# Feed-forward of a hybrid decoder trunk: the fourth weight sum of a seven-product pair written over its raw weights, t1 and t2 in units of their own

## The chip, the cores and the metric

The kernel runs on one core of a Trainium2 chip. Its time is device time in microseconds (us), the median of several executions. PE is the matrix engine (PEld its weight loads), DVE the vector engine, ACT the scalar engine, POOL GpSimd, and SP the queue that issues the weights' DMAs.

## The reference

Two layers over 256 positions of width 2048, all in float32: an mLSTM and state-space mixer in layer 0, block-sparse attention in layer 1, and after each a feed-forward of hidden width 5632, with norms and residuals around them. What the change touches is the feed-forward alone:

```python
def swiglu(x, w_gate, w_up, w_down):
    return (jax.nn.silu(x @ w_gate) * (x @ w_up)) @ w_down
...
    x = x + swiglu(rms_norm(x, norm_ffn[layer]), *ffn_params[layer])
```

## The kernel before

All weights stream once from HBM. A float32 product is done on PE in three passes: a weight is split into a rounded high part `wh` (a cast on ACT, L362) and the rest `wl` (a subtraction on DVE, L363), and activations are split in the same way, so that L399 to L401 multiply high with high, high with low, and low with high.

A feed-forward goes in three groups of 4, 4 and 3 hidden strips of 512 columns. For each strip `hidden` calls `block` with the gate and up weights; then `down` calls `block` twice, for q = 0 and q = 1, each with two strips of the down weights, and adds the four result banks to the residual `xres` (L865). A block walks in pairs of k tiles, after a plan of letters (PSPSPSPP for eight pairs, PSPSPP for six). Each pair needs two loads of 512 KB, raw a and raw b, of two k tiles each. A P pair is multiplied plainly: 24 matmuls. An S pair is done with seven products in place of eight (Strassen's scheme, in Winograd's form): 21 matmuls. It needs four sums of raw weights on DVE, here with the lines of before: L376 t1 = b(second half) - a(second half); L378 t3, over the second half of b; L379 t2, from b and t1; L381 t4, from a's first half and t2. t1 and t2 lie in one tile `sums`, t4 in half a tile `last`. a, b and `sums` are split whole, `last` by half.

Tiles come from rings of units of 4 KB for each partition. A unit is taken by turn and is free again once its last reader is done. Before, `raw` a, `raw` b, `sums` and `last` all take turns in one ring of eight units (tag raw0 four times, then raw1 four times); so an S pair takes four turns and a P pair two. `wh` and `wl` have rings of six each. A load can be issued when the unit of its turn is free, mostly after a split on DVE, and PE frees the `wh` and `wl` units. A list scheduler (Tile) puts all instructions of an engine in one fixed order when the kernel is built, by priorities and by when it thinks that units come free. SP, DVE, ACT and PE each run their own list in order; the first that must wait holds all behind it.

After the last S pair of a block come the pre-additions (L429 to L433) that free the four E banks. At the end of a block the four F banks are read by L865 (down) or by L850, L853 and L854 (hidden), before the next block's first products may write them.

Of the kernel before, what the change touches and what calls it, by code (L numbers as in the profile page):

```python
# [37 lines left out]
PLAN_H = {4: "PSPSPSPP", 3: "PSPSPP"}  # L38
MIXER = ({"wide": 2}, {"raw": 4, "wh": 3, "wl": 3}, {"blk": 8})
ATTN = ({"wide": 2}, {"qk": 8}, {"blk": 4}, {"raw": 4, "wh": 3, "wl": 3})  # L40
FFN = ({"raw0": 4}, {"wh0": 2}, {"wl0": 2}, {"raw1": 4, "wh1": 4, "wl1": 4}, {"skh": 3}, {"blk": 4})


def _host_constants():
# [15 lines left out]
def hybrid_trunk(ctx: ExitStack, tc: tile.TileContext, a: dict, out: bass.AP):  # L60
    nc = tc.nc
# [20 lines left out]
    def open_stage(name, pools):  # L82

        close_stage()
        stage["guards"], stage["pools"] = [], []
        for i, tags in enumerate(pools):
            guard = tc.tile_pool(name=f"{name}{i}", bufs=1, reuse_waits="tile")  # L90
            stage["guards"].append(guard)
            stage["pools"].append((guard.__enter__(), tags))

    def held_tile(tag, shape, name, dt=F32):
        for pool, tags in stage["pools"]:
            if tag in tags:
                return pool.tile(shape, dt, tag=tag, name=name, bufs=tags[tag])
        raise KeyError(tag)
# [254 lines left out]
    def weights(src, row, summed):  # L353

        def unit(kind, ring, name, dt=F32):
            turn[kind] = turn.get(kind, -1) + 1
            return held_tile(kind + ring[turn[kind] % len(ring)], [P, 2, STRIP], name, dt)

        def parts(of, n=2):
            h = unit("wh", "001111", "wh", F32R)  # L360
            l = unit("wl", "001111", "wl", F32R)
            nc.scalar.copy(h[:, :n, :], of[:, :n, :])  # L362
            nc.vector.tensor_sub(l[:, :n, :], of[:, :n, :], h[:, :n, :].bitcast(F32))  # L363
            return [(h[:, i, :], l[:, i, :]) for i in range(n)]

        raw = []
        for w, col in src:
            raw.append(unit("raw", "00001111", "raw"))
            nc.sync.dma_start(raw[-1], w[row:row + 2 * P, col:col + STRIP].rearrange("(a p) f -> p a f", p=P))
        with tc.high_priority(offset=800):  # L370
            if not summed:
                return [parts(r) for r in raw]
            a, b = raw
            sums = unit("raw", "00001111", "sums")
            last = unit("raw", "00001111", "last")
            nc.vector.tensor_sub(sums[:, 0, :], b[:, 1, :], a[:, 1, :])  # L376
            b21, b11 = parts(a)
            nc.vector.tensor_sub(b[:, 1, :], b[:, 0, :], b[:, 1, :])  # L378
            nc.vector.tensor_sub(sums[:, 1, :], b[:, 0, :], sums[:, 0, :])  # L379
            b22, t3 = parts(b)  # L380
            nc.vector.tensor_sub(last[:, 0, :], a[:, 0, :], sums[:, 1, :])  # L381
            t1, t2_ = parts(sums)
            t4, = parts(last, 1)
            return b21, b11, b22, t3, t1, t2_, t4

    def block(src, kt, row, nk, plan, after_sums=None, lead=1):
# [19 lines left out]
        for j in range(n):  # L406
            if plan[j] == "S":
                held[0] = True
                b21, b11, b22, t3, t1, t2_, t4 = weights(src, row + 2 * j * P, True)
                tok = lambda k, t: tuple(x[:, t * P:(t + 1) * P] for x in kt.parts(k))  # L410
                k2, k1 = 2 * j, 2 * j + 1
# [13 lines left out]
                if j == last_s:  # L425
# [8 lines left out]
                    if after_sums is not None:  # L434
                        after_sums(pre)
            else:
                group.append((j, weights(src, row + 2 * j * P, False)))
                if len(group) < lead and j < n - 1 and n - j <= lead:
                    continue
# [384 lines left out]
    def project_add(w, kt, nk, name, gcol):  # L824

        nx = KT("x" + name, KD, long)
        nx.sums = {j: None for j in range(KD // 2) if PLAN_X[j] == "S"}
        ss = cst.tile([P, NT, 4], F32, name="ss" + name)
        turn["acc"] = 4
        for s in range(4):  # L830
            banks = lin_a(w, s * STRIP, kt, nk)
            cs = slice(s * STRIP, (s + 1) * STRIP)
            for t in range(NT):
                nc.vector.tensor_add(xr_[t][:, cs], xr_[t][:, cs], banks[t])
            transpose_later(nx, s, [xr_[t][:, cs] for t in range(NT)], gcol, 1, 1 if s < 3 else 0)
            for t in range(NT):
                sumsq(ss[:, t, s:s + 1], xr_[t][:, cs])
        return nx, col_norm(name, ss)
# [51 lines left out]
    xt1, r1 = project_add(a["l0_w_out"], mixed, 32, "1", G_FFN0)  # L890
    open_stage("f", FFN)
    xt2 = KT("x2", KD, long)
# [44 lines left out]
    parts = (slice(0, P), slice(P, W3))  # L937
# [49 lines left out]
    xt3, r3 = project_add(a["l1_w_o"], oT, KD, "3", G_FFN1)  # L987
    open_stage("g", FFN)

# [56 lines left out]
```

## Time and profile before

| | us |
|---|---|
| median of 3 runs (2628.16 to 2630.83) | 2628.64 |
| the profiled execution, its time | 2630.54 |
| its span, first to last instruction | 2628.8 |
| first feed-forward, about | 783 to 1512 |
| second feed-forward with the tail, about | 1893 to 2629 |

A row of the waits says who waited, for whom, how long in total, how often, and the longest. A row of the timeline has start, duration, engine, line, operation, what it writes and reads, and in brackets how long the engine idled before it and what ended that. PE's matmuls overlap: one of 512 columns is listed with 0.39 us, but the next starts 0.23 us later. The granted PE clock is 0.997 of full speed over the whole span, and the 16 DMA engines are busy for 58% of each of the two feed-forwards.

### The profile page before, as it was taken

How to read it: one execution, taken by the hardware profiler on the slowest of the kernel's cores; microseconds unless marked ns; L12 is line 12 of the kernel's file. 1: busy time of each engine (PE TensorE's matmuls, PEld its weight loads, DVE VectorE, ACT ScalarE, POOL GpSimd, SP SyncE). 2: the span in 40 equal slices, each digit the busy share in tenths (PEclk: the TensorE clock that was granted, in tenths of full speed). 3: DMA queues.
4: the chain of work that ended last, by engine and by line, in shares of the span. 5: the costliest groups of instructions: out<-in, count | busy, mean ns of one | idle time of the engine just before them, and what ended most of it. 6: DMA issues, size and time to landing. Idle time of an engine off the chain costs nothing.

```text
span 2628.8 us, 33211 instructions
## 1 busy us (share of the span) xinstructions
PE 2581.6 (98%) x12231; PEld 2141.4 (81%) x12231; DVE 2069.3 (79%) x2768; ACT 1470.6 (56%) x2003; POOL 46.8 (2%) x97
## 2 busy tenths in 40 slices
PE   8999999999999999999999999999999999999998
PEld 7888888888887877787788788888888878887876
DVE  6675787765549998999899866566699889988998
ACT  5465665665446555555455556556565545554554
POOL 2000010000000000000000000000000000000000
PEclk9999999999999999999999999999999999999999
DMA  7566576566646655655565465555465556554654
GB/s 227 176 188 183 178 238 183 168 185 218 189 152 211 205 180 196 198 195 190 186 203 191 160 191 171 175 177 191 154 220 190 198 163 221 192 193 163 221 199 137
DMA packets 254771, 496.71 MB, mean 189 GB/s; under 512 B 15704, under 2 KB 16096, under 8 KB 254352
## 3 DMA queue, kind: packets, MB, share of 16 engines
q1 hardware_dynamic: 250816, 484.57, 57.7%
q0 software_dynamic: 2896, 8.51, 1.2%
q8 instruction: 96, 1.57, 0.2%
q10 hardware_dynamic: 896, 1.52, 0.2%
q14 instruction: 67, 0.55, 0.1%
HBM read 492.39 MB, written 2.14 MB: 188 GB/s over the span
## 4 chain that ended last, share of the span: by engine, by line
PE 74%; DVE 14%; DMA 6%; issue 4%; ACT 2%; SPq 0%; DVEq 0%; POOL 0%; ACTq 0%; POOLq 0%
PE acc_w L305 11%; PE acc_f L400 8%; PE acc_f L401 8%; PE acc_f L399 8%; PE acc_a L347 8%; PE acc_a L349 8%; PE acc_a L348 8%; DVE wl L363 7%; PE acc_w L309 6%; DMA raw<-in_l_ffn_down 3%; DMA raw<-in_l_ffn_up 3%; PE acc_e L399 2%; PE acc_e L401 2%; PE acc_e L400 2%; ACT wh L362 1%
## 5 line engine op out<-in xcount | busy, mean ns | idle before, releaser
L362 ACT CAST wh<-raw 128x1024 fp32r<-128x1024 f32 x528 | 546.0, 1053 | 416.8 <-PE acc_f L401 190.5
L290 DVE TENSOR_TENSOR wl<-raw,wh 128x1024 fp32r<-128x1024 f32 (+1 forms) x385 | 470.0, 1221 | 334.2 <-ACT wh L289 330.1
L363 DVE TENSOR_TENSOR wl<-raw,wh 128x1024 fp32r<-128x1024 f32 x528 | 636.7, 1223 | 86.0 <-ACT wh L362 82.7
L289 ACT CAST wh<-raw 128x1024 fp32r<-128x1024 f32 (+1 forms) x385 | 403.1, 1047 | 388.9 <-PE acc_a L349 175.7
L399 PE MATMUL acc_f<-wh,x 128*128 128x512 f32 x1012 | 396.1, 393 | 8.3 <-DVE xres L865 6.4
L401 PE MATMUL acc_f<-wh,x 128*128 128x512 f32 x1012 | 395.5, 391 | 0.0
L400 PE MATMUL acc_f<-wl,x 128*128 128x512 f32 x1012 | 395.4, 391 | 0.0
L399 PEld LDWEIGHTS acc_f<-wh,x 128*128 128x128 f32 x1012 | 190.1, 188 | 51.8 <-issue 8.0
L401 PEld LDWEIGHTS acc_f<-wh,x 128*128 128x128 f32 x1012 | 190.8, 189 | 39.7
L400 PEld LDWEIGHTS acc_f<-wl,x 128*128 128x128 f32 x1012 | 190.6, 188 | 39.1
L305 PE MATMUL acc_w<-xa,wh 128*128 128x512 f32 x768 | 209.5, 400 | 1.1 <-DVE xa L169 1.1
L305 PEld LDWEIGHTS acc_w<-xa,wh 128*128 128x128 f32 x768 | 140.1, 190 | 27.3 <-ACT wh L289 1.5
L347 PE MATMUL acc_a<-wh,xa 128*128 128x512 f32 x384 | 151.2, 394 | 0.0
L349 PE MATMUL acc_a<-wh,xa 128*128 128x512 f32 x384 | 151.0, 393 | 0.0
L348 PE MATMUL acc_a<-wl,xa 128*128 128x512 f32 x384 | 150.0, 391 | 0.0
L305 PE MATMUL acc_w<-x,wh 128*128 128x512 f32 x512 | 137.9, 399 | 0.0
L363 DVE TENSOR_TENSOR wl<-sums,wh 128x1024 fp32r<-128x1024 f32 x98 | 119.9, 1223 | 3.7 <-ACT wh L362 3.2
L309 PE MATMUL acc_w<-xa,wl 128*128 128x256 f32 x768 | 122.0, 283 | 0.0
L309 PEld LDWEIGHTS acc_w<-xa,wl 128*128 128x128 f32 x768 | 110.5, 191 | 6.7
L362 ACT CAST wh<-sums 128x1024 fp32r<-128x1024 f32 x98 | 102.7, 1048 | 15.3 <-PE acc_e L401 7.8
L305 PEld LDWEIGHTS acc_w<-x,wh 128*128 128x128 f32 x512 | 93.3, 189 | 17.7
L362 ACT CAST wh<-last 128x512 fp32r<-128x512 f32 x98 | 60.8, 620 | 82.5 <-DVE last L381 59.1
(318 smaller groups left out, 4768.5 us busy)
## 6 DMA issues: line engine op xcount, KB each, us to landing
raw<-in_l_w_in SPq DMA_DIRECT2D x191, 512.0 KB, 3.7
raw<-in_l_ffn_gate SPq DMA_DIRECT2D x176, 512.0 KB, 4.4
raw<-in_l_ffn_up SPq DMA_DIRECT2D x176, 512.0 KB, 4.9
raw<-in_l_ffn_down SPq DMA_DIRECT2D x176, 512.0 KB, 5.2
raw<-in_l_w_qkv SPq DMA_DIRECT2D x96, 512.0 KB, 3.6
raw<-in_l_w_out SPq DMA_DIRECT2D x64, 512.0 KB, 4.6
raw<-in_l_w_o SPq DMA_DIRECT2D x32, 512.0 KB, 4.0
rows<-scr POOLq DMA_DIRECT2D x10, 512.0 KB, 5.8
```

The lines of the kernel that those rows point to most:

```text
L289: nc.scalar.copy(wh[:, ks, :], raw[:, ks, :])
L290: nc.vector.tensor_sub(wl[:, ks, :], raw[:, ks, :], wh[:, ks, :].bitcast(F32))
L305: nc.tensor.matmul(banks[f], wh[:, kk, f * P:(f + 1) * P], kt.both(k0 + kk), start=k0 + kk == 0, stop=False, skip_group_check=True)
L309: nc.tensor.matmul(banks[f][:, :T], wl[:, kk, f * P:(f + 1) * P], kt.parts(k0 + kk)[0], start=False, stop=k0 + kk == nk - 1, skip_group_ch ...
L347: nc.tensor.matmul(banks[t], xh[:, ts], wh[:, kk, :], start=k == 0, stop=False)
L348: nc.tensor.matmul(banks[t], xh[:, ts], wl[:, kk, :], start=False, stop=False)
L349: nc.tensor.matmul(banks[t], xl[:, ts], wh[:, kk, :], start=False, stop=k == nk - 1)
L362: nc.scalar.copy(h[:, :n, :], of[:, :n, :])
L363: nc.vector.tensor_sub(l[:, :n, :], of[:, :n, :], h[:, :n, :].bitcast(F32))
L399: nc.tensor.matmul(dst, ah, bh, start=start, stop=False)
L400: nc.tensor.matmul(dst, ah, bl, start=False, stop=False)
L401: nc.tensor.matmul(dst, al, bh, start=False, stop=stop)
```

## The change

`last` goes: t4 is written over the first half of a, and split from there. `sums` gets two units of its own, and the raw ring keeps six. The eight units of 4 KB stay eight. One line fewer stands in the code, so L376, L378, L379, L381 and L865 of before are L375, L377, L378, L380 and L864 now.

```diff
-FFN = ({"raw0": 4}, {"wh0": 2}, {"wl0": 2}, {"raw1": 4, "wh1": 4, "wl1": 4}, {"skh": 3}, {"blk": 4})
+FFN = ({"raw0": 4}, {"wh0": 2}, {"wl0": 2}, {"raw1": 2, "sum0": 2, "wh1": 4, "wl1": 4}, {"skh": 3}, {"blk": 4})
...
         for w, col in src:
-            raw.append(unit("raw", "00001111", "raw"))
+            raw.append(unit("raw", "000011", "raw"))
...
             a, b = raw
-            sums = unit("raw", "00001111", "sums")
-            last = unit("raw", "00001111", "last")
+            sums = unit("sum", "0", "sums")
             nc.vector.tensor_sub(sums[:, 0, :], b[:, 1, :], a[:, 1, :])
             b21, b11 = parts(a)
             nc.vector.tensor_sub(b[:, 1, :], b[:, 0, :], b[:, 1, :])
             nc.vector.tensor_sub(sums[:, 1, :], b[:, 0, :], sums[:, 0, :])
             b22, t3 = parts(b)
-            nc.vector.tensor_sub(last[:, 0, :], a[:, 0, :], sums[:, 1, :])
+            nc.vector.tensor_sub(a[:, 0, :], a[:, 0, :], sums[:, 1, :])
             t1, t2_ = parts(sums)
-            t4, = parts(last, 1)
+            t4, = parts(a, 1)
```

What the scheduler makes of it is seen in the lists of the engines. The numbers in the names rise in the order in which the code makes the tiles.

The first place is SP's list in the second feed-forward, first group, q = 1: the loads of its fifth to eighth pairs. Before:

```order
L369 DMA raw_18525<-in_l1_ffn_down 128x2x512
L369 DMA raw_18527<-in_l1_ffn_down 128x2x512
L369 DMA raw_18561<-in_l1_ffn_down 128x2x512
L369 DMA raw_18563<-in_l1_ffn_down 128x2x512
L369 DMA raw_18657<-in_l1_ffn_down 128x2x512
L369 DMA raw_18659<-in_l1_ffn_down 128x2x512
L369 DMA raw_18621<-in_l1_ffn_down 128x2x512
L369 DMA raw_18623<-in_l1_ffn_down 128x2x512
```

And the same loads now:

```order
L369 DMA raw_18459<-in_l1_ffn_down 128x2x512
L369 DMA raw_18461<-in_l1_ffn_down 128x2x512
L369 DMA raw_18495<-in_l1_ffn_down 128x2x512
L369 DMA raw_18497<-in_l1_ffn_down 128x2x512
L369 DMA raw_18554<-in_l1_ffn_down 128x2x512
L369 DMA raw_18556<-in_l1_ffn_down 128x2x512
L369 DMA raw_18590<-in_l1_ffn_down 128x2x512
L369 DMA raw_18592<-in_l1_ffn_down 128x2x512
```

Before, the eighth pair's loads (18657, 18659) stand ahead of the seventh's (18621, 18623); now each load stands in the order of its use.

The second place is DVE's list in the first feed-forward, first group, q = 1, about its fourth to sixth pairs (the fourth and sixth are S pairs). Before, from the split of raw 8949 (third pair), whose end lets the load of raw 9068 (sixth pair) be issued, to the split of raw 8985 (b of the fourth pair):

```order
L363 TENSOR_TENSOR wl_8956<-raw_8949,wh_8955 128x1024
L363 TENSOR_TENSOR wl_8991<-raw_8983,wh_8990 128x1024
L381 TENSOR_TENSOR last_8988<-raw_8983,sums_8987 128x512
L363 TENSOR_TENSOR wl_9002<-sums_8987,wh_9001 128x1024
L363 TENSOR_TENSOR wl_9006<-last_8988,wh_9005 128x512
L376 TENSOR_TENSOR sums_9070<-raw_9068,raw_9066 128x512
L865 TENSOR_TENSOR xres1_5690<-xres1_5690,pre_8770 128x512
L363 TENSOR_TENSOR wl_8997<-raw_8985,wh_8996 128x1024
```

The same now, from the split of raw 8933, which lets raw 9051 be loaded:

```order
L363 TENSOR_TENSOR wl_8940<-raw_8933,wh_8939 128x1024
L363 TENSOR_TENSOR wl_8974<-raw_8967,wh_8973 128x1024
L380 TENSOR_TENSOR raw_8967<-raw_8967,sums_8971 128x512
L363 TENSOR_TENSOR wl_8980<-raw_8969,wh_8979 128x1024
L363 TENSOR_TENSOR wl_8989<-raw_8967,wh_8988 128x512
L363 TENSOR_TENSOR wl_9018<-raw_9013,wh_9017 128x1024
L375 TENSOR_TENSOR sums_9053<-raw_9051,raw_9049 128x512
```

The fourth pair's b (raw 8985, now 8969) was split behind the first sum of the sixth pair; now it is split ahead of it, with t4 and a split of the fifth pair.

The third place is DVE's list in the first feed-forward, last group, where q = 0 ends and q = 1 has begun: the residual's sums over q = 0 and the second and fourth pairs of q = 1. Before:

```order
L865 TENSOR_TENSOR xres0_5689<-xres0_5689,pre_12660 128x512
L363 TENSOR_TENSOR wl_12820<-raw_12808,wh_12819 128x1024
L865 TENSOR_TENSOR xres0_5689<-xres0_5689,acc_f_12496 128x512
L381 TENSOR_TENSOR last_12811<-raw_12806,sums_12810 128x512
L363 TENSOR_TENSOR wl_12825<-sums_12810,wh_12824 128x1024
L363 TENSOR_TENSOR wl_12829<-last_12811,wh_12828 128x512
L376 TENSOR_TENSOR sums_12897<-raw_12895,raw_12893 128x512
L865 TENSOR_TENSOR xres1_5690<-xres1_5690,pre_12661 128x512
L378 TENSOR_TENSOR raw_12895<-raw_12895 128x512
L865 TENSOR_TENSOR xres1_5690<-xres1_5690,acc_f_12489 128x512
L363 TENSOR_TENSOR wl_12901<-raw_12893,wh_12900 128x1024
```

And now, from the fourth pair's first sum on:

```order
L375 TENSOR_TENSOR sums_12849<-raw_12847,raw_12845 128x512
L363 TENSOR_TENSOR wl_12772<-raw_12761,wh_12771 128x1024
L380 TENSOR_TENSOR raw_12759<-raw_12759,sums_12763 128x512
L363 TENSOR_TENSOR wl_12777<-sums_12763,wh_12776 128x1024
L363 TENSOR_TENSOR wl_12781<-raw_12759,wh_12780 128x512
L377 TENSOR_TENSOR raw_12847<-raw_12847 128x512
L378 TENSOR_TENSOR sums_12849<-raw_12847,sums_12849 128x512
L864 TENSOR_TENSOR xres0_5689<-xres0_5689,pre_12613 128x512
L363 TENSOR_TENSOR wl_12852<-raw_12845,wh_12851 128x1024
L864 TENSOR_TENSOR xres0_5689<-xres0_5689,acc_f_12451 128x512
L380 TENSOR_TENSOR raw_12845<-raw_12845,sums_12849 128x512
L864 TENSOR_TENSOR xres1_5690<-xres1_5690,pre_12614 128x512
```

The fourth pair's first sum and the splits of t1, t2 and t4 stood between the residual's sums or behind two of them; now they stand ahead of all three rows with `xres` that are shown. Two more sums of `xres1`, the second over an F bank (acc_f_12444), follow directly.

## The prediction

> **What bounds the kernel now.** I read the page's engine row first, then the stretches of the two feed-forwards, and then who PE waits for in each.
>
> ```profile
> span 2628.8 us, 33211 instructions
> PE 2581.6 (98%) x12231; PEld 2141.4 (81%) x12231; DVE 2069.3 (79%) x2768; ACT 1470.6 (56%) x2003; POOL 46.8 (2%) x97
> 783.00:1512.00 729.00, 714.48 (x3168) 581.43 (x3167) 657.43 (x826) 406.28 (x477) 1.38 (x2) 1.00 0.58 191
> 1893.00:2629.00 736.00, 712.77 (x3136) 578.63 (x3134) 658.75 (x826) 403.86 (x468) 1.79 (x3) 0.99 0.58 190
> ```
>
> PE sets the time. The change touches only the two feed-forwards (the last two rows: length, then busy time of PE, PEld, DVE, ACT, POOL), and there PE idles 729.0 - 714.5 = 14.5 us and 736.0 - 712.8 = 23.2 us, the second with the kernel's tail in it. No change to the weights' buffers can bring more than these 37.7 us. What PE waits for (us in total, times, longest), three rows of the first feed-forward and the largest of the second:
>
> ```profile
> PE acc_f L400 <- DVE wl L363: 4.7, 2, 3.0
> PE p_tr L223 <- DVE h L854: 3.5, 5, 1.1
> ...
> PE acc_f L399 <- DVE xres L865: 0.8, 3, 0.3
> ...
> PE acc_f L399 <- DVE xres L865: 7.2, 9, 2.1
> ```
>
> Only the first row is a wait for weights. The others are for DVE's other work: a down bank added to the residual (L865), a hidden block's h (L854). DVE is 90% busy here (657.4 of 729.0), so what holds DVE reaches PE later under another name. What holds DVE is the loads:
>
> ```profile
> DVE sums L376 <- DMA raw<-in_l_ffn_down: 21.9, 11, 4.2
> DVE sums L376 <- DMA raw<-in_l_ffn_up: 11.4, 13, 1.9
> ACT wh L362 <- DMA raw<-in_l_ffn_down: 26.1, 8, 4.9
> SPq L369 <- DVE wl L363: 1137.2, 389, 18.8
> DMA to landing us min/median/max: 3.4/4.7/9.9
> ```
>
> The last two rows: SP waits for a split to free a unit before almost every load, and a load lands 3.4 to 9.9 us after its issue. DVE takes its work in order, so a sum (L376) whose load is late holds everything behind it.
>
> **The change part by part.** It removes no instruction and adds none: four sums (L376, L378, L379, L381) and four splits (L362 with L363) for each seven-product pair stay. L381 now writes over one of its own operands, and L378 does that already, at the same mean:
>
> ```profile
> L378 DVE TENSOR_TENSOR raw<-raw 128x512 f32<-128x512 f32 x98 | 67.5, 689 | 0.2
> L381 DVE TENSOR_TENSOR last<-raw,sums 128x512 f32<-128x512 f32 x98 | 67.5, 688 | 0.1
> ```
>
> That is 0 us (bounds 98 x 1 ns either way). The fourth sum must now come after a's own split, where the order before had it anyway: 0. Unit a is held through the split of t1 and t2 and that of t4, which stand right behind the fourth sum: it is freed 1.13 + 0.60 = 1.7 us later (paces of a whole and a half operation, from the rows at 1014.48 and 2541 below), and the loads' places count that. The eight units stay eight; what changes is which split frees which load, and so the order of loads on SP and of work on DVE. Three kinds of place gain.
>
> *First, the sum in front of a split that PE needs* (second half of a down pass, first feed-forward, twice):
>
> ```profile
> 1014.48 2.35 DVE L363 TENSOR_TENSOR wl<-raw,wh 128x1024 fp32r<-128x1024 f32 x2
> 1018.49 0.69 DVE L363 TENSOR_TENSOR wl<-last,wh 128x512 fp32r<-128x512 f32 x1
> 1021.22 0.69 DVE L376 TENSOR_TENSOR sums<-raw 128x512 f32<-128x512 f32 x1 [2.04 <-DMA raw<-in_l_ffn_down]
> 1023.70 0.50 PE L400 MATMUL acc_f<-wl,skh 128*128 128x512 f32 x1 [1.68 <-DVE wl L363]
> 1285.51 0.50 PE L400 MATMUL acc_f<-wl,skh 128*128 128x512 f32 x1 [3.03 <-DVE wl L363]
> ```
>
> The first split of the row at 1014.48 frees the late load's unit at about 1015.6; the load lands 5.6 us later; DVE has 3.4 us of other work and then stands, with the split that PE needs behind the sum. In the new order that split, the split of t4 and one more stand ahead of the sum. Gain 1.68 + 3.03 = 4.7 us; if the load is later than those three splits cover (1.1 + 0.6 + 1.1 us), part of it stays: bounds 2 and 4.7.
>
> *Second, loads stuck in SP's queue* (second feed-forward, twice):
>
> ```profile
> 2143.29 1.22 DVE L363 TENSOR_TENSOR wl<-raw,wh 128x1024 fp32r<-128x1024 f32 x1 [5.02 <-ACT wh L362]
> 2159.59 0.57 PE L399 MATMUL acc_f<-wh,x 128*128 128x512 f32 x1 [2.07 <-DVE xres L865]
> 2405.46 1.23 DVE L363 TENSOR_TENSOR wl<-raw,wh 128x1024 fp32r<-128x1024 f32 x1 [4.92 <-ACT wh L362]
> 2418.79 0.47 PE L399 MATMUL acc_f<-wh,x 128*128 128x512 f32 x1 [1.09 <-DVE xres L865]
> 2422.46 0.60 PE L399 MATMUL acc_f<-wh,x 128*128 128x512 f32 x1 [2.04 <-DVE xres L865]
> ```
>
> ACT's cast waited for a load (the ACT row above), because SP held it behind two loads that were not yet allowed. In the new order they are issued in the order of their use. DVE stood 5 us and then worked without a gap until PE waited for it: gain 2.07 + 1.09 + 2.04 = 5.2 us, bounds 3 and 5.2.
>
> *Third, the first sum of a down pass*, whose four loads were freed in one burst:
>
> ```profile
> 952.00 0.69 DVE L376 TENSOR_TENSOR sums<-raw 128x512 f32<-128x512 f32 x1 [3.44 <-DMA raw<-in_l_ffn_down]
> 969.15 0.44 PE L223 MATMUL p_tr<-ident,h 128*128 128x128 f32 x2 [1.13 <-DVE h L854]
> 975.02 0.88 PE L223 MATMUL p_tr<-ident,h 128*128 128x128 f32 x6 [0.64 <-DVE h L854]
> 2541.21 0.69 DVE L376 TENSOR_TENSOR sums<-raw 128x512 f32<-128x512 f32 x1 [4.16 <-DMA raw<-in_l_ffn_down]
> 2541.81 1.22 DVE L363 TENSOR_TENSOR wl<-raw,wh 128x1024 fp32r<-128x1024 f32 x1
> 2551.31 0.47 PE L399 MATMUL acc_f<-wh,hb 128*128 128x512 f32 x1 [1.03 <-DVE pre L850]
> 2558.36 0.44 PE L223 MATMUL p_tr<-ident,h 128*128 128x128 f32 x2 [1.11 <-DVE h L854]
> 2564.23 0.88 PE L223 MATMUL p_tr<-ident,h 128*128 128x128 f32 x6 [0.64 <-DVE h L854]
> ```
>
> In the new order, at those paces, 2.5 and 4 us more DVE work stand between the release of the load and its sum, against waits of 3.44 and 4.16. Gain 1.13 + 0.64 + 1.03 + 1.11 + 0.64 = 4.6 us, bounds 2 and 4.6. Together 14.5 us.
>
> **What is late next.** At the end of a down half the new order puts the next pair's L376 and several splits ahead of the residual sums that free PE's banks. There are ten such places (q = 0 to 1 six times, down to hidden four times). The price, by hand, for the worst one (first feed-forward, last group): from the matmul that frees the split's buffer to the matmul that needs the bank there are 18 matmuls in the built program, at the 0.227 us between the starts of two (5 in 1.14 us below) 4.1 us. DVE's way is a cast 1.05, the split 1.13, and five operations at a pace of 0.60: 5.2 us. So 1.1 us late.
>
> ```profile
> L362 ACT CAST wh<-raw 128x1024 fp32r<-128x1024 f32 x528 | 546.0, 1053 | 416.8 <-PE acc_f L401 190.5
> ...
> 1011.63 0.39 PE L400 MATMUL acc_f<-wl,skh 128*128 128x512 f32 x1
> ...
> 1012.77 0.40 PE L399 MATMUL acc_f<-wh,ha 128*128 128x512 f32 x1
> ...
> 2376.28 0.47 PE L399 MATMUL acc_f<-wh,hb 128*128 128x512 f32 x1 [0.58 <-DVE xres L865]
> ```
>
> The same sum gives 0.4 us at three, 0.06 at two and -0.1 at four. It leaves out the hops between engines: for the place of the last row it gives -0.25, and PE waited 0.58. I take 0.7 us for them (0.5 to 0.9 fit the rows of before): 1.8 + 3 x 1.1 + 2 x 0.8 + 4 x 0.6 = 9.1 us. These places cost already 0.8 and 7.2 - 5.2 = 2.0 us, so 6.3 us are new (bounds 4 and 9 from the hops alone). The sum is 14.5 - 6.3 = 8.2 us. The profiled execution took 2630.5 us; 2622.3 is left. The three runs have a median 1.9 us below it, so the forecast is **2620.5 us**.
>
> [...]
>
> **The rivals.** *No change to measure:* a measurement tells 0.2%, 5.3 us, from nothing. The regrouped units remain eight, and DVE's 657 us of work still must pass beside PE. If the sums merely move DVE's idle time, half of the 14.5 us comes back: 14.5 / 2 - 6.3 = 1 us, 2627.7 us. For it: most waits of L376 (24 of them) reach no PE wait today; against it: 7 of the 10 PE waits in the rows above follow one.
>
> *Slower:* at the ten ends of down halves L376 now stands ahead of the residual sums. If its load lands later than about 4.7 us after issue, each further microsecond is one more at each place. Two stretches of before show what such loads take (median us to landing):
>
> ```profile
> raw<-in_l_ffn_down SPq DMA_DIRECT2D x4, 512.0 KB, 4.7
> ...
> raw<-in_l_ffn_down SPq DMA_DIRECT2D x4, 512.0 KB, 7.3
> ```
>
> The first row is from 1465 to 1478 us, the loads of just such a place; the second from 926 to 952, a burst. At 5.5 us the new cost is about 6.3 + 10 x 0.8 = 14.3 us and eats the gain; at 7.3 it is 6.3 + 26 = 32.3 us, 2628.6 + 17.8 = 2646.4 us. Against it: the loads there are now released one by one, not four at once.
>
> *It does not do what it says:* if the scheduler had kept SP's order, nothing would change; the rows printed above rule that out.
>
> **How the numbers follow.** Forecast, faster by 5 to 16 us: 0.60. No change: 0.28. Slower: 0.12. Low end: all of the 14.5 us and no new cost gives 2628.6 - 14.5 = 2614.1; I go to 2613 for the small waits that may go too. High end: gains at their lower bounds (2 + 3 + 2 = 7 us) and a new cost of 9 give 2 us more than 2628.6. So 2613 to 2630.
>
> **What would show it.** DVE's waits at L376 (now L375) for loads fall from 33.3 us to under 15; the waits near 1022, 1283, 2143 and 2405 are gone; PE waits for xres more often than 12 times, each around 1 us; PE's busy time stays near 2582. It is wrong if the loads' median at the ends of down halves rises over 5.5 us, or if PE's waits for wl or h stay although DVE's waits for loads went.

## The result, and the profile after

The changed kernel takes **2605.42 us**, the median of 4 runs (2601.99 to 2606.75), beside 2628.40 us (2627.97 to 2630.83, 4 runs) for the kernel before: a ratio of 0.9909, 95% interval 0.9892 to 0.9926. It gains 23.0 us where 8 were forecast, and lies outside the range.

The page of the changed kernel first, as read before (busy time of each engine; its profiled execution took 2606.75 us):

```profile
span 2605.0 us, 33393 instructions
PE 2571.0 (99%) x12231; PEld 2141.0 (82%) x12231; DVE 2067.6 (79%) x2768; ACT 1477.3 (57%) x2003; POOL 46.8 (2%) x97
```

PE's busy time fell too, by 10.6 us, although it does the same 12231 matmuls. Where the time went is seen in stretches that are cut at the first and the last matmul of each feed-forward. First before (length, then busy time of PE, PEld, DVE, ACT and POOL, granted clock, DMA share, GB/s):

```profile
0.00:790.00 790.00, 779.98 (x3972) 660.16 (x3972) 515.23 (x780) 441.47 (x699) 43.64 (x92) 1.00 0.62 190
790.00:1508.60 718.60, 707.08 (x3131) 575.61 (x3132) 653.01 (x815) 401.67 (x466) 0.69 (x1) 1.00 0.59 193
1508.60:1898.30 389.70, 386.54 (x2020) 330.69 (x2018) 243.72 (x351) 225.31 (x376) 0.69 (x1) 1.00 0.57 176
1898.30:2617.90 719.60, 707.63 (x3113) 574.90 (x3112) 653.90 (x816) 398.83 (x459) 0.69 (x1) 1.00 0.58 190
```

And the same four stretches after:

```profile
0.00:790.80 790.80, 779.83 (x3971) 660.15 (x3971) 514.91 (x780) 441.42 (x699) 43.61 (x92) 1.00 0.62 190
790.80:1499.00 708.20, 703.98 (x3130) 575.75 (x3131) 652.00 (x815) 404.73 (x466) 0.69 (x1) 1.00 0.62 196
1499.00:1888.70 389.70, 386.23 (x2016) 330.43 (x2014) 244.20 (x352) 225.30 (x376) 0.69 (x1) 1.00 0.57 176
1888.70:2594.40 705.70, 700.61 (x3115) 574.62 (x3115) 653.09 (x815) 402.59 (x459) 0.69 (x1) 1.00 0.62 194
```

The two feed-forwards are 10.4 and 13.9 us shorter, together 24.3; the stretch between them is equal to the tenth. PE's listed idle time in them fell only from 11.5 + 12.0 = 23.5 us to 4.2 + 5.1 = 9.3 us. The other 10.1 us came out of its *busy* time, so idle time is a poor measure here.

What waits now, for the whole execution (us in total, times, longest; L375 is the first sum, L376 before):

```profile
DVE sums L375 <- DMA raw<-in_l_ffn_down: 5.6, 7, 1.4
...
DVE sums L375 <- DMA raw<-in_l_ffn_up: 4.5, 5, 2.0
...
PE acc_e L399 <- DVE wl L363: 6.0, 6, 1.5
...
PE acc_f L399 <- DVE wl L363: 1.5, 4, 0.6
```

DVE's waits for loads at the first sum fell from 33.3 to 10.1 us. PE's waits for h (L854), for xres (L865) and for pre (L850) are gone altogether. In their place PE waits six times for `wl` of the first S pair behind the end of a down half.

The loads themselves land no faster: from issue to landing they take 4.5 us at the median, 4.7 before.

To count what the rows of idle time hide, I took PE's matmuls of the feed-forwards in order and added up by how much each starts later than its pace (0.227 us behind the one before; behind a transpose, which has 128 columns in place of 512, a quarter of that, 0.06 us). The 0.06 us are my estimate, and low: in both traces a transpose starts 0.11 us (median) behind the one before, so some 5 to 7 us of the row of the smaller ones, before and after alike, are no stalls. This ledger gives 55.3 us before and 30.9 us after:

| stalls of PE in the two feed-forwards, us | before | after | change | forecast |
|---|---|---|---|---|
| the ten waits that the three kinds of place named | 16.1 | 0.0 | -16.1 | -14.5 |
| the ends of down halves (beside those ten) | 5.7 | 13.9 | +8.1 | +6.3 |
| matmuls at half the granted clock | 4.9 | 0.0 | -4.9 | 0 |
| other stalls over 0.15 us | 11.8 | 3.0 | -8.7 | 0 |
| all smaller ones | 16.8 | 14.0 | -2.8 | 0 |
| sum | 55.3 | 30.9 | -24.4 | -8.2 |

The two rows that were forecast came out at -8.0 us against -8.2, the one 1.6 us larger, the other 1.8. That they agree so closely in sum is luck. What was missing are the three rows below them, 16.4 us.

The third row of the ledger, the half clock, is seen in the windows of before around one of the named waits (columns as above, the granted clock third from the end):

```profile
1282.00:1285.50 3.50, 0.48 (x3) 0.06 (x1) 2.48 (x4) 1.04 (x1) 0.00 (x0) 1.00 1.01 381
1285.50:1286.30 0.80, 0.79 (x3) 0.49 (x4) 0.80 (x2) 0.00 (x0) 0.00 (x0) 0.81 0.48 184
1286.30:1288.90 2.60, 2.60 (x8) 2.02 (x8) 2.60 (x4) 0.00 (x0) 0.00 (x0) 0.50 0.08 32
```

PE paused for 3.03 us; then the granted clock stood at 0.50. What that does to matmuls is plainest in before's timeline behind the pause at 2420:

```profile
2423.28 0.63 PE L401 MATMUL acc_f<-wh,x 128*128 128x512 f32 x1
2423.71 0.63 PE L399 MATMUL acc_f<-wh,x 128*128 128x512 f32 x1
2424.14 0.63 PE L400 MATMUL acc_f<-wl,x 128*128 128x512 f32 x1
...
2426.40 0.39 PE L400 MATMUL acc_e<-wl,x 128*128 128x512 f32 x1
2426.64 0.40 PE L401 MATMUL acc_e<-wh,x 128*128 128x512 f32 x1
```

They start every 0.43 us instead of 0.23. This pause cost its own length and then some 1.6 us more (4.9 us in the ledger for three such pauses), which no row lists as a wait: PE is busy. The same stands behind the waits of 2.07 and 2.04 us at 2157 and 2420, not behind the 1.68 us at 1022.

The second row of the ledger is seen in the timeline of after where q = 1 begins, second feed-forward, second group (first DVE's rows, then two of PE's):

```profile
2352.07 0.69 DVE L375 TENSOR_TENSOR sums<-raw 128x512 f32<-128x512 f32 x1
2352.67 1.22 DVE L363 TENSOR_TENSOR wl<-raw,wh 128x1024 fp32r<-128x1024 f32 x1
2353.81 0.68 DVE L864 TENSOR_TENSOR xres<-xres,acc_f 128x512 f32<-128x512 f32 x1
...
2357.09 0.69 DVE L375 TENSOR_TENSOR sums<-raw 128x512 f32<-128x512 f32 x1 [1.40 <-DMA raw<-in_l_ffn_down]
2357.70 1.22 DVE L363 TENSOR_TENSOR wl<-raw,wh 128x1024 fp32r<-128x1024 f32 x1
...
2362.38 0.68 DVE L864 TENSOR_TENSOR xres<-xres,pre 128x512 f32<-128x512 f32 x1
2362.99 1.22 DVE L363 TENSOR_TENSOR wl<-raw,wh 128x1024 fp32r<-128x1024 f32 x1
...
2362.41 0.39 PE L398 MATMUL acc_e<-wh,hb 128*128 128x512 f32 x1
2364.26 0.50 PE L399 MATMUL acc_e<-wl,hb 128*128 128x512 f32 x1 [1.46 <-DVE wl L363]
```

Two first sums stand here 5 us apart. The second waits 1.40 us for its load; from 2357.09 on DVE works without a gap, and the split that PE needs next comes 1.46 us too late. DVE waits 0.4 to 1.4 us in this way where the q = 1 of each of the six groups begins, 5.4 us together, and PE then waits 6.2 us for a split. In five of the six PE's wait is DVE's wait and less than 0.1 us more (1.46 behind 1.40 here). So as I read it, nearly all of this is a load that is later than the work in front of it, and little of it is the order of DVE's work alone.

### The profile page after: what moved, and what is told of

Read it like the earlier page. It is cut to its first block, busy times and chain, and to the rows that moved or that the text cites. A ratio compares the mean times of both kernels' runs of the same rounds, so it can differ in the third digit from the quotient of the medians.

```text
span 2605.0 us, 33393 instructions
## 1 busy us (share of the span) xinstructions
PE 2571.0 (99%) x12231; PEld 2141.0 (82%) x12231; DVE 2067.6 (79%) x2768; ACT 1477.3 (57%) x2003; POOL 46.8 (2%) x97
## 4 chain that ended last, share of the span: by engine, by line
PE 86%; DVE 7%; DMA 3%; issue 2%; ACT 1%; POOL 0%; ACTq 0%; SPq 0%; POOLq 0%; DVEq 0%
PE acc_f L399 11%; PE acc_f L400 11%; PE acc_f L398 11%; PE acc_w L305 11%; PE acc_a L347 8%; PE acc_a L349 8%; PE acc_a L348 8%; PE acc_w L309 6%; DVE wl L363 3%; PE acc_e L398 3%; PE acc_e L399 3%; PE acc_e L400 3%; PE p_tr L223 2%; DMA raw<-in_l_ffn_down 1%; ACT wh L362 1%
## 5 line engine op out<-in xcount | busy, mean ns | idle before, releaser
L362 ACT CAST wh<-raw 128x1024 fp32r<-128x1024 f32 (+1 forms) x626 | 606.9, 986 | 462.7 <-PE acc_f L400 229.3
L363 DVE TENSOR_TENSOR wl<-raw,wh 128x1024 fp32r<-128x1024 f32 (+1 forms) x626 | 702.2, 1137 | 93.1 <-ACT wh L362 91.7
L290 DVE TENSOR_TENSOR wl<-raw,wh 128x1024 fp32r<-128x1024 f32 (+1 forms) x385 | 469.9, 1221 | 334.6 <-ACT wh L289 330.7
L289 ACT CAST wh<-raw 128x1024 fp32r<-128x1024 f32 (+1 forms) x385 | 403.1, 1048 | 389.0 <-PE acc_a L349 175.0
L399 PE MATMUL acc_f<-wl,ha 128*128 128x512 f32 x256 | 100.0, 391 | 1.1 <-DVE wl L363 1.1
```

What stands on the lines that cost most here:

```text
L289: nc.scalar.copy(wh[:, ks, :], raw[:, ks, :])
L290: nc.vector.tensor_sub(wl[:, ks, :], raw[:, ks, :], wh[:, ks, :].bitcast(F32))
L399: nc.tensor.matmul(dst, ah, bl, start=False, stop=False)
```

## The experiments

The theory taken into them (A): what counts is how much DVE work the built program puts between the split that frees a load's unit and the first use of that load, its *cover*. It is counted in the built lists with the paces of the prediction's rows (1.13 us a whole split, 0.60 the smaller operations). Before, a load lands in 4.7 us at the median, and a load with less cover than that can stop DVE. The rivals: the number of units that loads can hold (B), SP's order (C, counted as the places where a load stands in SP's list just ahead of one that is used earlier), and later the time that unit a is held by t4 (D). The expectations of the first eight kernels count covers under 4 us. By their results the count under 5 us orders the kernels better, so the last four use that; it was chosen after the first eight were known. Lines of the experiments are those of before. Medians are of 4 runs (10 for the fourth); the kernel before, run beside them, had 2627.8 us with the first four, 2629.9 with the next four and 2628.6 with the last four:

| kernel | covers under 4 / 5 us | places out of order on SP | DVE's waits for loads at the first sum, us | median, us | ratio, 95% interval |
|---|---|---|---|---|---|
| before | 31 / 56 | 55 | 33.3 | 2628.4 | |
| the change | 7 / 39 | 17 | 10.1 | 2605.4 | 0.9892 to 0.9926 |
| 1: t4 over a alone | 57 / 69 | 59 | 49.0 | 2642.9 | 1.0044 to 1.0075 |
| 2: t1, t2 in own units alone | 14 / 32 | 55 | 5.3 | 2595.6 | 0.9866 to 0.9895 |
| 3: before, loads in order | 0 / 0 | 0 | 0 | 2598.3 | 0.9874 to 0.9907 |
| 4: seven raw units, one for sums | 51 / 57 | 36 | 50.6 | 2625.7 | 0.9987 to 1.0005 |
| 5: the change, loads in order | 7 / 39 | 0 | 9.5 | 2607.5 | 0.9901 to 0.9930 |
| 6: before, loads in order among themselves | 0 / 0 | 0 | 0 | 2588.4 | 0.9826 to 0.9855 |
| 7: as 2, loads in order | 8 / 8 | 0 | 0.2 | 2587.6 | 0.9827 to 0.9856 |
| 8: the change, one unit for sums | 7 / 11 | 17 | 9.6 | 2596.5 | 0.9859 to 0.9892 |
| 9: before, first sum tied | 0 / 0 | 50 | 0 | 2595.7 | 0.9854 to 0.9884 |
| 10: the change, first sum tied | 0 / 0 | 14 | 0 | 2593.2 | 0.9843 to 0.9878 |
| 11: as 1, first sum tied | 0 / 0 | 89 | 0 | 2593.4 | 0.9848 to 0.9879 |
| 12: as 4, first sum tied | 0 / 0 | 32 | 0 | 2597.9 | 0.9864 to 0.9894 |

### The halves of the change, one order, one more unit

**1.** t4 written over a, the ring of eight kept:

```diff
-            last = unit("raw", "00001111", "last")
...
-            nc.vector.tensor_sub(last[:, 0, :], a[:, 0, :], sums[:, 1, :])
+            nc.vector.tensor_sub(a[:, 0, :], a[:, 0, :], sums[:, 1, :])
...
-            t4, = parts(last, 1)
+            t4, = parts(a, 1)
```

> One half of the change: t4 is written over a, but t1 and t2 still take their turns in the ring of eight units with the loads (three turns for an S pair instead of four). Three theories, each scaled on 2628.4 us before and 2605.4 us after. (A, cover) What counts is how much DVE work the built program puts between the split that frees a load's unit and the first use of that load; loads with under 4 us of it are short covers. Before has 31 of them, after 7, so about 1 us each. This kernel has 57: 2655 us, in any case slower than before. (B, places) What counts is how many units the loads hold: 528 loads of 724 turns in 8 units are 5.8 before, 6 after, and 528 of 626 in 8 are 6.7 here: at or below 2605 us. (C, SP's order) What counts is a load that stands in SP's list ahead of one that is used earlier: 55 such places before, 17 after, 59 here: 2630 us, as before.

**2.** The two units for t1 and t2, and `last` kept:

```diff
-FFN = ({"raw0": 4}, {"wh0": 2}, {"wl0": 2}, {"raw1": 4, "wh1": 4, "wl1": 4}, {"skh": 3}, {"blk": 4})
+FFN = ({"raw0": 4}, {"wh0": 2}, {"wl0": 2}, {"raw1": 2, "sum0": 2, "wh1": 4, "wl1": 4}, {"skh": 3}, {"blk": 4})
-            raw.append(unit("raw", "00001111", "raw"))
+            raw.append(unit("raw", "000011", "raw"))
...
-            sums = unit("raw", "00001111", "sums")
-            last = unit("raw", "00001111", "last")
+            sums = unit("sum", "0", "sums")
+            last = unit("raw", "000011", "last")
```

> The other half: t1 and t2 have two units of their own, the raw ring has six, and t4 keeps half a tile of its own, by turns in that ring (three turns for an S pair). (A, cover) 14 short covers against 31 before and 7 after: 2612 us, most of the gain. (B, places) 528 of 626 turns in 6 units are 5.1 for the loads, fewer than the 5.8 of before: 2628 us or slower. (C, SP's order) 55 places out of order, as before: 2628 us.

**3.** Before, with every load of a feed-forward pinned behind all that SP was given earlier:

```diff
-            nc.sync.dma_start(raw[-1], w[row:row + 2 * P, col:col + STRIP].rearrange("(a p) f -> p a f", p=P))
+            tc.keep_in_program_order(nc.sync.dma_start(raw[-1], w[row:row + 2 * P, col:col + STRIP].rearrange("(a p) f -> p a f", p=P)))
```

> Before, with its ring of eight units and four turns for an S pair, but SP's loads are tied to the order of their use (an order of issue on SP, no wait is added). (A, cover) No load has a cover under 4 us, and none under 6: 2598 us, faster than after. (B, places) 5.8 units for the loads as before: 2628 us. (C, SP's order) 0 places out of order against 17 after: 2595 us.

**4.** Seven raw units:

```diff
-FFN = ({"raw0": 4}, {"wh0": 2}, {"wl0": 2}, {"raw1": 2, "sum0": 2, "wh1": 4, "wl1": 4}, {"skh": 3}, {"blk": 4})
+FFN = ({"raw0": 4}, {"wh0": 2}, {"wl0": 2}, {"raw1": 3, "sum0": 1, "wh1": 4, "wl1": 4}, {"skh": 3}, {"blk": 4})
-            raw.append(unit("raw", "000011", "raw"))
+            raw.append(unit("raw", "0000111", "raw"))
```

> The change, with seven raw units and one unit for t1 and t2 in place of six and two. (A, cover) 51 short covers: 2649 us, slower than before. (B, places) Seven units for the loads against six: faster than after, under 2605 us. (C, SP's order) 36 places out of order: 2617 us. If one unit for t1 and t2 is itself too few, it comes out slower by all of them, and PE or DVE would be seen waiting at L376 for PE or ACT, not for a DMA.

Theory A tells the two fast kernels from the two others and has the third at its 2598 us; elsewhere its sizes are too large (2655 for 2642.9, 2612 for 2595.6, and 2649 for the fourth, which is no slower than before with 2625.7). B, the number of units, is wrong on all four: the kernel whose loads have 6.7 units is the slowest, that with 5.1 gains most. C is wrong on the second kernel, with 55 places out of order and 32 us faster than before. A seventh raw unit made the change 20 us slower, which speaks against too few units as well. **The change is a gain with a loss taken off it:** t1 and t2 in units of their own give 2628.4 - 2595.6 = 32.8 us, and t4 over a gives 2605.4 - 2595.6 = 9.8 us back (on the ring of eight 2642.9 - 2628.4 = 14.5 us). What the first kernel's DVE and PE wait for shows how (from 785 to 2620 us):

```profile
DVE sums L376 <- DMA raw<-in_l_ffn_down: 26.1, 14, 4.8
DVE sums L376 <- DMA raw<-in_l_ffn_up: 20.5, 17, 2.2
DVE sums L376 <- DMA raw<-in_l_ffn_gate: 2.4, 3, 0.9
...
PE p_tr L223 <- DVE h L854: 14.2, 20, 1.6
```

The in-place sum itself cost nothing (689 ns each at the mean, 688 before); the first sums wait half as long again as in before (49.0 against 33.3 us), and PE waits for h twenty times, since DVE is late with all that stands behind them.

### Order, and one unit for the sums

**5, 6, 7.** Each load of a feed-forward is tied to the load before it, no other instruction of SP; in the change, in before, and in the second experiment:

```diff
-            nc.sync.dma_start(raw[-1], w[row:row + 2 * P, col:col + STRIP].rearrange("(a p) f -> p a f", p=P))
+            with tc.issue_after(turn["dma"]) if "dma" in turn else ExitStack(): turn["dma"] = nc.sync.dma_start(raw[-1], w[row:row + 2 * P, col:col + STRIP].rearrange("(a p) f -> p a f", p=P)).ins
```

> The change, and the feed-forwards' loads tied to the order of their use on SP (each behind the load before it, no other instruction of SP tied). (A, cover) 7 short covers, as in the change: 2605 us. (C, SP's order) 0 places out of order instead of 17: about 2596 us. Between the two would mean that both count.

> As the third experiment, but the loads are tied to each other alone, so that the first loads of a feed-forward may pass other transfers on SP. If the 4.6 us that the stretch between the feed-forwards took longer there (394.3 against 389.7 us) come from the tie to those transfers, this gives 2598.3 - 4.6 = 2593.7 us; if they come from the loads' order itself, 2598 us.

> As the second experiment (t1 and t2 in two units of their own, t4 in half a tile in the raw ring), with the loads tied to each other in the order of their use. (A, cover) 8 short covers against 14: some 6 us under the 2595.6 us, but no lower than the order alone gives, about 2593 us. (C, SP's order) 0 against 55 places: far under 2595.6 us, if the 55 cost anything; they can cost at most what is above the lowest, some 3 us.

**8.** The change with `"sum0": 1` for `"sum0": 2`:

> The change with one unit for t1 and t2 in place of two; the raw ring keeps its six. Its use is to read the kernel with seven raw units and one sum unit (2625.7 us). (A, cover) 7 short covers, as in the change: 2605 us, so that the seventh raw unit is what cost 20 us there. Rival: one sum unit is too few, the next t1 waits for the split of the last: about 2625 us here too, with DVE waiting at L376 for ACT or PE.

The fifth says that SP's order by itself is not the cause: none out of order, the covers as in the change, and the time as in the change. In the sixth the tie took DVE's short covers along (0 of 528), and it is 40 us faster than before, with no unit changed. It came 5 us under its expectation, since the third kernel's extra time lay not only between the feed-forwards but ahead of both: PE paused 2.59 us there for the first casts, twice, and the half clock followed (mean granted clock 0.997 in the third kernel, 0.999 in the sixth). The sixth and the seventh are the fastest kernels here, 17 to 18 us below the change. The eighth misses by theory A's count under 4 us (2605 for 2596.5) and by the rival (2625): one unit for the sums is not too few, and the seventh raw unit is what hurt the fourth kernel. Its count under 5 us (11 for 39) goes the right way, but its first sums wait 9.6 us, as in the change; so the sum of these waits alone doesn't set the time, and where they fall must count too. The same shows in the fourth kernel, which waits 50.6 us and is as fast as before.

The ledger of the sixth kernel is 12.8 us, against 55.3 and 30.9: its feed-forwards take 698.9 and 696.9 us, the ends of its down halves cost 0.2 us. In the feed-forwards the change gained 24.3 us and the sixth kernel 42.4.

### The first sum alone

**9 to 12.** One line of the order is added in four kernels (before, the change, the first and the fourth experiment): the first sum of an S pair is tied behind the last split of the pair before it in DVE's list, an order of issue that adds no wait (the scheduler then builds the rest of DVE's list anew):

```diff
-            nc.vector.tensor_sub(l[:, :n, :], of[:, :n, :], h[:, :n, :].bitcast(F32))
+            turn["split"] = nc.vector.tensor_sub(l[:, :n, :], of[:, :n, :], h[:, :n, :].bitcast(F32)).ins
...
-            nc.vector.tensor_sub(sums[:, 0, :], b[:, 1, :], a[:, 1, :])
+            with tc.issue_after(turn["split"]) if "split" in turn else ExitStack(): nc.vector.tensor_sub(sums[:, 0, :], b[:, 1, :], a[:, 1, :])
```

> Before, with its units and ring, but the first sum of an S pair (L376) is tied behind the last split of the pair before it in DVE's list (order of issue alone, no wait added). SP's loads are left to the scheduler. (A, cover) No load has under 5 us of DVE work between its release and its first use (56 before, 39 in the change): the floor that the loads in order gave, 2588 us, within 4. (C, SP's order) 50 places out of order against 55 before: no better than 2620 us. (D, hold) Nothing is held for a shorter time than before: about 2628 us.

> The change, with the first sum tied behind the last split of the pair before it. (A, cover) No load with under 5 us instead of 39: 2588 us, and PE's waits for wl behind the ends of the down halves (6.0 us at acc_e) are gone. (C) 14 places out of order against 17: 2603 us. (D, hold) Unit a is held through the split of t4 as in the change; what that costs, at most the 10 us between the change and the sums alone, stays: 2598 us or more.

> The first experiment (t4 over a, t1 and t2 in the ring of eight; 2642.9 us), with the first sum tied behind the last split of the pair before it. (A, cover) No load with under 5 us instead of 69: 2588 us. (C) 89 places out of order, more than in any other kernel: over 2640 us. (D, hold) Writing t4 over a cost 15 us there; if by holding a, it costs about that here too: 2603 us.

> Seven raw units and one unit for t1 and t2 (2625.7 us), with the first sum tied behind the last split of the pair before it. (A, cover) No load with under 5 us instead of 57: 2588 us, and the number of units is no matter. (C) 32 places out of order: 2615 us. (B, places) The seventh unit lets loads run further ahead, so it should come out under the others with the sum tied.

Four kernels that were up to 37.5 us apart (2642.9, 2628.4, 2625.7, 2605.4) come within 4.7 us of each other. C falls as an account of what sets these kernels apart: 89 places out of order go with 2593.4 us. Nor do loads that land sooner explain it: at the median they take 4.8 and 5.0 us in the ninth and the eleventh, 4.7 before. D falls: t4 over a, the tie in place, is no slower than before with the tie (2593.4 and 2593.2 against 2595.7). B falls: seven units are the slowest of the four. A names the cause and is 5 to 10 us too low; 1.6 to 4.7 us of that lie between the feed-forwards in the ninth, eleventh and twelfth (391.3, 391.3 and 394.3 us, for 389.6 in the sixth), where the half clock fell, and some 5 to 8 us are stalls in the feed-forwards that I did not follow, but for 2.9 us of the ninth's, which fall in the two blocks behind loads that still pass each other on SP. What PE waits for in the ninth kernel and then in the tenth, up to the end of the second feed-forward (the row with L834 belongs to the stage between the two):

```profile
PE acc_f L399 <- DVE xres L865: 1.9, 4, 0.9
PE p_tr L223 <- DVE xres L834: 1.1, 2, 0.6
PE acc_f L400 <- DVE wl L363: 1.1, 3, 0.5
PE p_tr L223 <- DVE h L854: 0.6, 1, 0.6
```

```profile
PE p_tr L223 <- DVE xres L834: 1.1, 2, 0.6
PE acc_f L399 <- ACT wh L362: 0.3, 1, 0.3
```

In the ninth, ring and units are those of before, and PE's waits for h fell from 5.9 us to 0.6, those for xres from 8.1 to 1.9. So most of these waits came from where the first sums stood in the list. Whether it was their waits for loads, or the work that stood behind them in any case, these four kernels don't separate, since the tie takes both away. In the tenth the waits for `wl` behind the down halves are gone too, and with them the change's second row of the ledger (13.9 us, now 0.1).

## Why the prediction was wrong

**PE is the bound, the change acts in the feed-forwards alone:** right; nothing else moved by more than 0.8 us.

**"No change to the weights' buffers can bring more than these 37.7 us":** wrong. The figure was listed idle time, and part of it lies outside the feed-forwards' matmuls. Between them 23.5 us are listed and 55.3 us lost by the ledger, and the sixth kernel, by order alone, gained 42.4 us there. No new division of the buffers brought more than 32.8 us here, so none broke the figure; but it was no bound. A matmul is listed with 0.39 us and paced at 0.227, so each pause is listed some 0.16 us short, one under 0.16 us isn't listed at all, and a matmul at half clock counts as busy. For the same reason PE's busy time didn't stay near 2582 us.

**The fourth sum in place costs 0:** right as an operation (experiments 10 and 11 against 9). But the prediction then put the longer hold of unit a down as a matter of the loads' places and gave it no price of its own, and with the scheduler free to place the first sum this half of the change costs 9.8 to 14.5 us.

**The three kinds of place:** all ten waits went, 16.1 us for 14.5; the 1.6 us are the same short listing. For the second kind the cause was named too narrowly, as SP's queue. In the ninth kernel the loads still pass each other at these very places, and PE loses 1.3 and 1.6 us in the two blocks in place of 4.6 and 4.5. So with that order left as it was, two thirds of PE's loss went, with the first sums and the half clock. The queue's order is a part all the same: DVE still stands 2.72 and 2.98 us there for casts whose loads are late (5.02 and 4.92 before).

**What is late next:** the place was right and the size near, 8.1 us for 6.3 at the ends of down halves; the mechanism was not. The forecast had the order of DVE's work make the residual's sums late, with PE waiting for `xres`. PE waits for `wl` instead, and at the six starts of q = 1 5.4 of its 6.2 us are DVE's own waits for the first sum's load. That is the slower rival's mechanism, a load that lands later than its cover, and it came without later landings. So the near agreement of the numbers is luck.

**The step that failed is the sum of the gains, "Together 14.5 us".** It took the list of three kinds of place for complete and left every other stall of before standing. Missing were 4.9 us at half clock behind three of the ten waits themselves, 8.7 us of other listed stalls and 2.8 us of small ones, 16.4 us in all. The rivals' text had even counted that 24 waits of L376 "reach no PE wait today". As I read it they did, later and under another name: DVE is 90% busy here, regains little, and what it lost at a sum came out at an h or at a bank some microseconds on. The ninth kernel fits: ring and units are those of before, DVE's 33.3 us of waits at the first sums are gone, and it is 32.7 us faster. The fourth, with 50.6 us of them and before's time, says that they don't all cost alike. And the low end of 2613 us had 1.1 us for "the small waits that may go too", where 11.5 us went.

**The signs named beforehand:** waits at the first sum under 15 us (10.1) and the four waits gone came true; PE waiting more often for xres (not once in the list) and PE busy near 2582 us (2571.0) did not. Of the two signs of being wrong one appeared: PE's waits for wl stayed (5.3 us before, 7.5 after, at other places) though DVE's waits for loads fell. The other did not, as loads around the ends of down halves take 4.5 us at the median.

## What to carry to other kernels

Where an engine that works in order is nearly full and feeds the one that bounds, a wait of it can cost even if nobody waits for it at that moment; look at the wait itself, not only at the stalls that follow in sight (33.3 us of such waits gone went with 32.7 us in the ninth kernel, though 17.3 us more of them cost nothing in the fourth). In a schedule made at build time, count the work between the release of a buffer and the first use of what is loaded into it, and compare it with the time that a load takes to land in the trace: tying one instruction a little later gained as much here (32.7 us) as the best new division of the buffers (32.8), and tying the loads in order more (40.0). And read a pipelined engine's losses from start to start: here its rows of idle time showed 23.5 of the ledger's 55.3 us.

## What the hardware showed

In the fourteen profiles a granted clock of 0.50 followed all eight pauses of 2.04 to 3.03 us inside the feed-forwards and at their start, one of two pauses of 1.9 us, and one of six of 1.41 to 1.68 us (the one of 1.63). Pauses of 2.10 to 2.27 us where the first feed-forward ends had it in five of fourteen (not behind the 2.11 us of before and the 2.10 us of the change), in kernels that are alike there, so the length of a pause alone does not settle it; what else does, the profiles do not show. Behind all these pauses it lasted 3.4 us, and it made the stretch between the feed-forwards 391.3 us long in place of 389.7.
